# Experts of a mixture layer taken slice by slice in turn: three with 128 slots, five with 64 slots in plain fp32

## The chip, the cores and the metric

The kernel runs on one core of a Trainium2 chip. The metric is device time in microseconds (us) of one execution. A core has five engines that work side by side, each through its own instructions in order: PE (matmuls; PEld is its weight load), DVE and ACT (element-wise work), POOL, and SP, whose queue issues the transfers (DMA) from the chip's memory. Tiles lie in 128 partitions; accumulators of PE lie in eight banks (PSUM), one tile of 128 x 512 fp32 each.

## The reference, cut to what matters

Two layers run over 256 latent tokens of width 1024 and 256 context tokens. The end of the second layer, and 352 of the 490 MB that the program loads, is a mixture of eight experts of which each token uses two:

```python
def moe_ffn(h, w_router, b_router, w1, w3, w2):
    logits = (h @ w_router).astype(jnp.float32) + b_router.astype(jnp.float32)
    top_v, top_i = lax.top_k(logits, TOP_K)          # TOP_K = 2, N_EXPERTS = 8
    gates = jax.nn.softmax(top_v, axis=-1)
    comb = jnp.sum(jax.nn.one_hot(top_i, N_EXPERTS, dtype=jnp.float32) * gates[..., None], axis=-2)
    ...
    for e in range(N_EXPERTS):
        y = y + comb[..., e:e + 1] * swiglu(h, w1[e], w3[e], w2[e])
    return y

def swiglu(h, w1, w3, w2):                           # w1, w3: 1024 x 3584, w2: 3584 x 1024
    return (jax.nn.silu(h @ w1) * (h @ w3)) @ w2
```

## The kernel before, in words

The first part of the program (attention, dense layer, recurrent block) ends near 965 us of the profiled execution and is not touched. Then the router's scores are made (`lg`), each token's two experts are found, `asg` (token x expert, 0 or 1), `pos` (the token's place in its expert's list, by a matmul with a triangle) and `cnt` (how many tokens an expert has) are computed, and the experts follow.

An expert's hidden width of 3584 is cut into `NST` = 7 slices of 512. A slice has 12 units of weights, 128 x 1024 fp32 or 512 KB each: four of w1, four of w3 and four of w2. `up` computes both products of a slice, ACT takes Silu of the first (`msil`), DVE multiplies, PE transposes the result (`pgt`), and `w2_step` multiplies it by w2 one slice later, so that in slice n stand the w1 and w3 of slice n and the w2 of slice n - 1, then the transposes of slice n (`hidden`).

There are two kinds of expert. A *heavy* one has room for 128 tokens (slots). Its operands are split into two fp32r parts each: ACT casts a unit (`whi`, L354), DVE subtracts (`wlo`, L365), and PE makes three products (L1880 to L1882, and L1813 to L1815 for w2). The raw buffer of a unit is free once DVE has subtracted; up to `SB` = 5 units are split ahead. A *light* one (`LIGHT`) has `CAP` = 64 slots and multiplies in plain fp32 (L1793): two matmuls of 64 columns of weights work side by side on the two halves of the array, nothing is split, and the raw buffer is free only after its matmuls. Expert 0 is always the first, heavy; experts 1 to 7 are sorted by the length of their lists (`sort`, on DVE), the three longest are heavy, the four shortest light, and `RANK` deals them out alternately: heavy, light, heavy, light and so on, each with its seven slices in one piece.

Tokens are collected by matmuls with a 0/1 matrix: `gather` (eight per heavy expert) and `small_gather` (eight for all light ones together, into `xs`), after `picks` and `small_picks` on DVE. `turn` transposes an expert's matrix, `lift` scales its result, and `combine` (four per expert) adds it to the tokens. These are put into `side`, from which `step()` takes one piece after every second pair of units, four times per slice.

The class `Stream` loads the units in the order in which PE will want them. `load` issues transfers on SP as long as a raw buffer is free; SP then waits, in order, until the buffer's former user is done. Later tiles (`xs`, `xe`, `ysb`) lend their space to the stream before they are needed (`AG`). Which expert a load reads is taken from `order`, the sorted table, through a register (`expert`).

## Time and profile before

| | |
|---|---|
| time, median of 3 runs (lowest, highest) | 1849.22 us (1842.72, 1854.35) |
| the profiled execution | 1849.13 us, of which the span of its records is 1847.4 us |
| PE busy | 1770.6 us, 96% of the span |
| DVE busy | 1185.7 us, 64% |
| ACT busy | 859.7 us, 47% |
| DMA | 489.92 MB, mean 265 GB/s over the span |
| mean granted clock of PE | 0.981 of full |

All times inside the program count from the span's start. In rows of instructions, the first number is the start, the second the duration, both in us; `x4` is a count of merged instructions; the bracket names how long the engine stood idle before, and what ended that. `out<-in` are the program's names for tiles.

### The profile page before, as it was taken

How to read it: one execution, taken by the hardware profiler on the slowest of the kernel's cores; microseconds unless marked ns; L12 is line 12 of the kernel's file. 1: busy time of each engine (PE TensorE's matmuls, PEld its weight loads, DVE VectorE, ACT ScalarE, POOL GpSimd, SP SyncE). 2: the span in 40 equal slices, each digit the busy share in tenths (PEclk: the TensorE clock that was granted, in tenths of full speed). 3: DMA queues.
4: the chain of work that ended last, by engine and by line, in shares of the span. 5: the costliest groups of instructions: out<-in, count | busy, mean ns of one | idle time of the engine just before them, and what ended most of it. 6: DMA issues, size and time to landing. Idle time of an engine off the chain costs nothing.

```text
span 1847.4 us, 26663 instructions
## 1 busy us (share of the span) xinstructions
PE 1770.6 (96%) x10067; PEld 1357.1 (73%) x10067; DVE 1185.7 (64%) x1751; ACT 859.7 (47%) x1263; POOL 189.3 (10%) x195
## 2 busy tenths in 40 slices
PE   8999899999999999998778999999999999999996
PEld 6887568888788889877677886578755886578753
DVE  4784676876666448699987882188614983088611
ACT  4434655422222235776735762177413771167500
POOL 1001242100000003244650000000000000000000
PEclk9999999999999999999887999999999999999999
DMA  7444611464665323232565979999999999999996
GB/s 304 163 150 147 206 58 46 160 209 148 235 217 193 100 83 115 80 103 91 195 249 189 355 279 387 418 419 420 419 419 420 419 420 416 420 420 419 415 419 281
DMA packets 95257, 489.92 MB, mean 265 GB/s; under 512 B 10512, under 2 KB 16016, under 8 KB 56464
## 3 DMA queue, kind: packets, MB, share of 16 engines
q1 hardware_dynamic: 94976, 488.01, 68.4%
q8 instruction: 81, 1.33, 0.3%
q14 instruction: 56, 0.46, 0.1%
q10 hardware_dynamic: 144, 0.13, 0.0%
HBM read 487.05 MB, written 1.05 MB: 264 GB/s over the span
## 4 chain that ended last, share of the span: by engine, by line
PE 76%; DVE 11%; DMA 8%; ACT 2%; issue 2%; POOL 1%; SPq 0%; DVEq 0%; ACTq 0%; POOLq 0%
PE ph L1793 8%; DMA raw<-moe_d 7%; PE ph L1882 5%; PE ph L1880 5%; PE ph L1881 5%; PE psa L454 4%; PE psa L455 4%; PE psa L456 4%; PE py L1793 3%; PE py L1813 3%; PE py L1815 3%; PE py L1814 3%; DVE wlo L365 2%; PE pF L454 2%; PE pF L455 2%; PE pF L456 2%
## 5 line engine op out<-in xcount | busy, mean ns | idle before, releaser
L365 DVE TENSOR_TENSOR wlo<-raw,whi 128x1024 fp32r<-128x1024 f32 x480 | 575.4, 1237 | 158.5 <-ACT whi L354 157.1
L354 ACT CAST whi<-raw 128x1024 fp32r<-128x1024 f32 x484 | 490.9, 1048 | 206.5 <-PE pF L455 49.8
L1793 PE MATMUL ph<-raw,xs 128*64 128x256 f32 x1792 | 207.7, 383 | 1.4 <-DMA raw<-moe_d 1.4
L1882 PE MATMUL ph<-wlo,xe 128*128 128x512 f32 x448 | 178.4, 398 | 6.0 <-DVE wlo L365 6.0
L1880 PE MATMUL ph<-whi,xe 128*128 128x512 f32 x448 | 180.8, 404 | 2.5 <-ACT whi L354 2.5
L1881 PE MATMUL ph<-whi,xe 128*128 128x512 f32 x448 | 177.4, 396 | 0.0
L1793 PEld LDWEIGHTS ph<-raw,xs 128*64 128x64 f32 x1792 | 123.3, 137 | 65.3 <-issue 4.5
L454 PE MATMUL psa<-hh,whi 128*128 128x512 f32 (+1 forms) x384 | 144.8, 377 | 0.0
L455 PE MATMUL psa<-hl,whi 128*128 128x512 f32 (+1 forms) x384 | 143.9, 375 | 0.7 <-DVE hl L705 0.6
L456 PE MATMUL psa<-hh,wlo 128*128 128x512 f32 (+1 forms) x384 | 143.4, 373 | 0.0
L1793 PE MATMUL py<-raw,mgs 128*64 128x512 f32 (+1 forms) x496 | 103.4, 556 | 5.0 <-DMA raw<-moe_d 4.5
L579 DVE SCALAR_TENSOR_TENSOR macc<-raw,c,macc 128x1024 f32<-128x1024 f32 x84 | 105.3, 1280 | 0.7
L1882 PEld LDWEIGHTS ph<-wlo,xe 128*128 128x128 f32 x448 | 85.9, 192 | 26.3 <-DVE wlo L365 7.6
L1910 DVE TENSOR_TENSOR msil<-msil,ph 128x256 f32<-128x256 f32 x28 | 11.8, 420 | 144.1 <-PE ph L1793 144.1
L1880 PEld LDWEIGHTS ph<-whi,xe 128*128 128x128 f32 x448 | 86.2, 192 | 20.0 <-ACT whi L354 3.0
L1881 PEld LDWEIGHTS ph<-whi,xe 128*128 128x128 f32 x448 | 86.2, 192 | 17.3
L1813 PE MATMUL py<-whi,mgh 128*128 128x512 f32 x224 | 87.6, 391 | 0.0
L1815 PE MATMUL py<-wlo,mgh 128*128 128x512 f32 x224 | 87.3, 390 | 0.0
L1814 PE MATMUL py<-whi,mgl 128*128 128x512 f32 x224 | 87.2, 389 | 0.0
L454 PEld LDWEIGHTS psa<-hh,whi 128*128 128x128 f32 x384 | 73.0, 190 | 14.3 <-issue 2.1
L455 PEld LDWEIGHTS psa<-hl,whi 128*128 128x128 f32 x384 | 73.1, 190 | 13.6 <-DVE hl L705 1.5
L456 PEld LDWEIGHTS psa<-hh,wlo 128*128 128x128 f32 x384 | 73.1, 190 | 12.7
(351 smaller groups left out, 3235.8 us busy)
## 6 DMA issues: line engine op xcount, KB each, us to landing
raw<-moe_d SPq DMA_DIRECT2D x302, 1024.0 KB, 15.3
raw<-f_d SPq DMA_DIRECT2D x66, 512.0 KB, 3.6
raw<-wm_d SPq DMA_DIRECT2D x64, 512.0 KB, 4.7
raw<-moe_d SPq DMA_DIRECT2D x64, 512.0 KB, 15.7
raw<-wmh_d SPq DMA_DIRECT2D x32, 512.0 KB, 8.1
raw<-qkv_d SPq DMA_DIRECT2D x24, 512.0 KB, 4.4
raw<-win_d SPq DMA_DIRECT2D x24, 512.0 KB, 3.6
raw<-gat_d SPq DMA_DIRECT2D x14, 512.0 KB, 3.7
```

The source lines that it names most:

```text
L354: self.nc.scalar.copy(hi, self.raws[i][0])
L365: eng.tensor_tensor(lo, self.take(key), hi.bitcast(F32), ALU.subtract)
L454: nc.tensor.matmul(o, w[0], x[0], start=first, stop=False)
L455: nc.tensor.matmul(o, w[0], x[1], start=False, stop=False)
L456: nc.tensor.matmul(o, w[1], x[0], start=False, stop=last)
L1793: nc.tensor.matmul(o[h], x, w[h], start=first, stop=last, skip_group_check=True)
L1813: nc.tensor.matmul(ys[e][n], x[0], w[0], start=b, stop=False)
L1814: nc.tensor.matmul(ys[e][n], x[1], w[0], start=False, stop=False)
L1815: nc.tensor.matmul(ys[e][n], x[0], w[1], start=False, stop=l)
L1880: nc.tensor.matmul(acc[part], xh[:, k], w[0], start=(k == 0), stop=False)
L1881: nc.tensor.matmul(acc[part], xl_[:, k], w[0], start=False, stop=False)
L1882: nc.tensor.matmul(acc[part], xh[:, k], w[1], start=False, stop=(k == 7))
```

## The change

The numbers of kinds and the order change. `FEW` = 5 experts are light, three are heavy, and `order` is used as sorted: places 0, 1 and 2 are heavy (expert 0 and the two longest lists), 3 to 7 light. Slices are no longer taken expert by expert: `turns` lists all 56 slices, first three of expert 0, then the 35 light ones in order with the other 18 heavy ones spread between them: `h h h l l h l l h l l h l l h l l h l h l l h ...`, with three light ones at the end. Heavy and light experts are thus open at the same time, so the accumulators are no longer taken from rotating pools: `bank` hands three banks round for w1 and w3, a light slice puts both of its halves of 256 columns into one of them, a fourth bank holds the light w2 sums and two hold the heavy ones.

As the first light loads come early, `sort` runs ahead of the first gathers, the rest of it (`permute`) after slice 0 as before, and the count of tokens is made beside `pos`. `gate` holds back loads that need `order` until `sort` has been written. `xs` and `ysb` lend less space. The small gathers, now 320 columns wide, move from slices 4 and 5 into slice 2, three per `step()`. `combine` of an expert starts two places after its last slice.

```diff
-RANK = (None, 3, 0, 4, 1, 5, 2, 6)
-LIGHT = (1, 3, 5, 7)
+FEW = 5
+HEAVY = tuple(range(NE - FEW))
+LIGHT = tuple(range(NE - FEW, NE))
+
+
+def turns():
+    h, l = ([(e, s) for e in k for s in range(NST)] for k in (HEAVY, LIGHT))
+    q = h[:3]
+    h = h[3:]
+    n = len(h)
+    for i, x in enumerate(l):
+        q.append(x)
+        while h and len(h) > n - n * (i + 1) // (len(l) - 3):
+            q.append(h.pop(0))
+    return q
+
+
+SEQ = turns()
...
-AG = (1,1)
+AG = (0, 1)
...
-        while self.dma_at < len(self.units) and n:
+        while self.dma_at < (len(self.units) if self.gate is None else self.gate) and n:
...
-    for p in range(NE):
-        for s in range(NST):
...
+    for n, (p, s) in enumerate(SEQ):
+        if p and st.gate is None:
+            st.gate = len(st.units)
...
-                once = [mp.tile([P, 2, UNIT], F32, name="raw", tag=n, bufs=b) for n, b in (("xs", 1), ("xe", 2))]
-                st.add_tiles(once, 2 * AG[0], True)
-                st.add_tiles([mp.tile([P, UNIT], F32, name="raw", tag="ysb", bufs=1)], AG[1])
+                once = mp.tile([P, max(2 * UNIT, KD * CAP * FEW)], F32, name="raw", tag="xs", bufs=1)
+                st.add_tiles([once[:, 0:2 * UNIT].rearrange("p (i n) -> p i n", i=2)], AG[0], True)
+                st.add_tiles([mp.tile([P, 2, UNIT], F32, name="raw", tag="xe", bufs=2)], AG[1], True)
...
+    nc.tensor.matmul(pp[:, 16:24], ones, asg[:, 0], start=False, stop=False)
+    nc.tensor.matmul(pp[:, 16:24], ones, asg[:, 1], start=False, stop=True)
...
+    sort()
+    st.gate = None
+    for k in range(KD):
+        gather(0, k)
...
+    banks_a, banks_u, turn_a = [psa("ph") for _ in range(4)], [psu("py") for _ in range(2)], [0]
+
+    def bank():
+        turn_a[0] += 1
+        return banks_a[turn_a[0] % 3]
...
     def step():
-        if side:
-            side.pop(0)()
+        for _ in range(rate[0]):
+            if side:
+                side.pop(0)()
...
-        acc = [psa("ph")[:, 0:NL], psa("ph")[:, 0:NL]]
+        acc = bank()
+        acc = [acc[:, 0:NL], acc[:, NL:512]]
...
+    for n, (e, s) in enumerate(SEQ):
+        while after and after[0][0] <= n:
+            p = after.pop(0)[1]
+            side[:0] = [lambda p=p, c=c: combine(p, c) for c in range(4)]
...
+        if n == 2:
+            side += [lambda t=t: small_picks(t) for t in range(2)]
+            side += [lambda k=k: small_gather(k) for k in range(KD)]
+        rate[0] = 3 if n == 2 else 1
+        sil = (small_up if e in LIGHT else up)(e, s)
...
```

Three places show how instructions move. On SP, the loads (`raw<-moe_d`) that stand ahead of the first use of `order`, and the first behind it; before, the table's first use comes 28 loads further on. Before, from the second load into a lent tile on:

```order
L289 DMA raw<-moe_d 128x2048 [waits DMAHW7_49]
L276 DMA raw<-moe_d 128x1024 [waits DMAHW0_49,DVE_49]
L276 DMA raw<-moe_d 128x1024 [waits DMAHW1_49]
L289 DMA raw<-moe_d 128x2048 [waits DMAHW2_49,DVE_49]
L289 DMA raw<-moe_d 128x2048 [waits DMAHW3_49,Pool_49]
L289 DMA raw<-moe_d 128x2048 [waits DMAHW4_49,PE_49]
L289 DMA raw<-moe_d 128x2048 [waits DMAHW5_49,DVE_49]
```

The change, from the same load on:

```order
L306 DMA raw<-moe_d 128x2048 [waits DMAHW7_49]
L306 DMA raw<-moe_d 128x2048 [waits DMAHW0_49,DVE_49]
L306 DMA raw<-moe_d 128x2048 [waits DMAHW1_49,Pool_49]
L306 DMA raw<-moe_d 128x2048 [waits DMAHW2_49,PE_49]
L306 DMA raw<-moe_d 128x2048 [waits DMAHW3_49,DVE_49]
L797 TENSOR_LOAD order [waits DVE_49]
```

The pair of half-size loads into a raw buffer and the lent `ysb` is gone, so that each later load stands behind a release of a buffer that is one pair of units later; and SP now reads `order` here.

On DVE, the start of the experts. Before, the eight subtractions of the first gathers follow the parts `hnl` of the tokens at once, and the sort (`key` to `order`) stands behind slice 0:

```order
L1643 TENSOR_SCALAR Pm<-con,pos,asg 128x128 x2
L1614 SCALAR_TENSOR_TENSOR hnl<-pR,nry,hnh 128x512 x3
L1667 SCALAR_TENSOR_TENSOR xe<-pg,mods_78,xe 128x128 x8
L1702 COPY cnt<-pcnt 128x8
L365 TENSOR_TENSOR wlo<-raw,whi 128x1024 x7
```

The change:

```order
L1657 COPY cnt<-ppos 128x8
L1662 TENSOR_SCALAR Pm<-con,pos,asg 128x128 x2
L1631 SCALAR_TENSOR_TENSOR hnl<-pR,nry,hnh 128x512 x3
L1719 TENSOR_SCALAR key<-con 128x8
L1720 SCALAR_TENSOR_TENSOR key<-cnt,key 128x8
L1722 TENSOR_TENSOR above<-key 128x49
L1724 TENSOR_REDUCE rank<-above 128x7
L1725 TENSOR_TENSOR perm<-rank,con 128x49
L1726 MEMSET srt 128x16
L1727 TENSOR_TENSOR permv<-perm,con 128x49
L1728 TENSOR_REDUCE srt<-permv 128x7
L1729 CAST order<-srt 128x8
```

Nine instructions stand between the tokens' parts and the eight `xe` subtractions now.

On PE, the w1 and w3 matmuls of a light slice (`ph<-raw,xs`; the waits for `DMAHW` are for loaded units). Before, the last two pairs of units and the first of w2:

```order
L1793 MATMUL ph<-raw,xs 64x256 [waits DMAHW7_49]
L1793 MATMUL ph<-raw,xs 64x256 x7
L1793 MATMUL ph<-raw,xs 64x256 [waits DMAHW0_49]
L1793 MATMUL ph<-raw,xs 64x256 x7
L1793 MATMUL py_10153<-raw,mgs 64x512 [waits DMAHW1_49,Activation_49]
```

The change, in a light slice behind a heavy one:

```order
L1816 MATMUL ph<-raw,xs 64x256 [waits DMAHW6_49]
L1816 MATMUL ph<-raw,xs 64x256 x3
L1816 MATMUL ph<-raw,xs 64x256 [waits DMAHW7_49,Activation_49]
L1816 MATMUL ph<-raw,xs 64x256 x7
L1836 MATMUL py<-whi,mgh 128x512
```

The last pair of w3 units waits for ACT as well.

## Rows read from the trace of the kernel before

**Rows 1.** The page: the DMA engines' share and rate in 40 equal slices.
```profile
DMA  7444611464665323232565979999999999999996
GB/s 304 163 150 147 206 58 46 160 209 148 235 217 193 100 83 115 80 103 91 195 249 189 355 279 387 418 419 420 419 419 420 419 420 416 420 420 419 415 419 281
```

**Rows 2.** DMA issues from 900 us on: count, KB of each, us to landing.
```profile
raw<-moe_d SPq DMA_DIRECT2D x302, 1024.0 KB, 15.3
raw<-moe_d SPq DMA_DIRECT2D x64, 512.0 KB, 15.7
raw<-w2l_d SPq DMA_DIRECT2D x4, 512.0 KB, 14.3
```

**Rows 3.** Stretches: us, busy us (count) of five engines, PE clock, DMA share, GB/s.
```profile
912.00:1037.00 125.00, 108.41 (x601) 96.27 (x600) 106.47 (x166) 71.39 (x100) 32.07 (x23) 0.86 0.64 247
1037.00:1045.00 8.00, 8.00 (x39) 6.65 (x38) 6.09 (x7) 5.41 (x7) 0.00 (x0) 1.00 1.04 368
1037.00:1115.00 78.00, 77.06 (x387) 63.13 (x387) 61.88 (x64) 52.35 (x62) 0.00 (x0) 1.00 0.81 298
1120.00:1800.00 680.00, 674.72 (x3881) 468.06 (x3881) 369.67 (x425) 311.50 (x397) 0.00 (x0) 0.99 1.01 419
1825.00:1832.00 7.00, 5.53 (x36) 2.09 (x32) 0.35 (x1) 0.74 (x2) 0.00 (x0) 1.00 0.67 266
1005.00:1010.00 5.00, 3.12 (x7) 2.48 (x8) 4.93 (x9) 1.04 (x1) 0.00 (x0) 0.50 0.18 29
```

**Rows 4.** Waits of SP's queue from 982 to 1115: us in total, times, longest.
```profile
SPq L289 <- DVE wlo L365: 108.2, 30, 16.2
```

**Rows 5.** Timeline of PE: transposes at the end of heavy (L1859) and light (L1854) slices.
```profile
1037.01 0.60 PE L1859 MATMUL pgt<-con,msil 128*128 128x128 f32 x4
...
1109.52 0.60 PE L1859 MATMUL pgt<-con,msil 128*128 128x128 f32 x4
...
1197.88 0.44 PE L1854 MATMUL pgt<-con,msil 128*128 128x128 f32 x2
...
1300.20 0.60 PE L1859 MATMUL pgt<-con,msil 128*128 128x128 f32 x4
...
1317.01 0.60 PE L1859 MATMUL pgt<-con,msil 128*128 128x128 f32 x4
...
1790.45 0.44 PE L1854 MATMUL pgt<-con,msil 128*128 128x128 f32 x2
...
1801.31 0.44 PE L1854 MATMUL pgt<-con,msil 128*128 128x128 f32 x2
```

**Rows 6.** Timeline: the sort on DVE (first row, row behind its last), PE's stop.
```profile
999.36 0.17 DVE L1724 TENSOR_SCALAR key<-con 128x8 f32<-128x8 f32 x1
...
1001.06 0.20 DVE L1738 TENSOR_TENSOR permv<-perm,cnt 128x49 f32<-128x49 f32 x1
...
1006.88 0.79 PE L1882 MATMUL ph<-wlo,xe 128*128 128x512 f32 x1 [4.90 <-DVE wlo L365]
```

**Rows 7.** Timeline of PE: small gathers, the first and the second.
```profile
1063.66 0.39 PE L1684 MATMUL pg<-Ps,hnh 128*128 128x256 f32 x1 [0.94 <-DVE Ps L1643]
...
1066.84 0.40 PE L1684 MATMUL pg<-Ps,hnh 128*128 128x256 f32 x2
...
1067.32 0.40 PE L1813 MATMUL py<-whi,mgh 128*128 128x512 f32 x1
```

**Rows 8.** Groups by line and form: ACT's casts and the light slices' Silu.
```profile
L354 ACT CAST whi<-raw 128x1024 fp32r<-128x1024 f32 x484 | 490.9, 1048 | 206.5 <-PE pF L455 49.8 <-issue 46.1 <-DMA raw<-moe_d 35.8
...
L1908 ACT ACTIVATE msil<-ph 128x256 f32<-128x256 f32 x28 | 10.8, 385 | 85.8 <-PE ph L1793 85.8
```

**Rows 9.** Timeline of the end: ACT's last copy, w2 behind it, last addition.
```profile
1829.61 0.37 ACT L1856 COPY mgs<-pgt 128x256 f32<-128x256 f32 x1 [7.55 <-PE pgt L1854]
...
1830.03 1.09 PE L1793 MATMUL py<-raw,mgs 128*64 128x128 f32 x16 [0.52 <-ACT mgs L1856]
...
1839.64 0.48 DVE L730 SCALAR_TENSOR_TENSOR xl<-pc,mods,xl 128x256 f32<-128x256 f32 x1 [0.59 <-PE pc L1830]
```

More of the change, by code (lines that the diff above doesn't have):

```diff
@@ L1635, in body @@
     nc.tensor.matmul(pp[:, 0:16], tri, asg.rearrange("p t e -> p (t e)"), start=True, stop=False)
-    nc.tensor.matmul(pp[:, 0:16], ones, asz[:, 0:2].rearrange("p t e -> p (t e)"), start=False, stop=True)
+    nc.tensor.matmul(pp[:, 0:16], ones, asz[:, 0:2].rearrange("p t e -> p (t e)"), start=False, stop=False)
+    nc.tensor.matmul(pp[:, 16:24], ones, asg[:, 0], start=False, stop=False)
+    nc.tensor.matmul(pp[:, 16:24], ones, asg[:, 1], start=False, stop=True)
     nc.vector.tensor_copy(pos, pp[:, 0:16].rearrange("p (t e) -> p t e", t=2))
+    nc.vector.tensor_copy(cnt, pp[:, 16:24])
     xe, PT, pms = {}, {}, {}
-    col = [0] + [1 + RANK[p] for p in range(1, NE)]
     def hot(o, slots, p, t, gate=None):
-        c = col[p]
+        c = p
         nc.vector.tensor_scalar(
@@ L1672, in small_picks @@
         if t == 0:
-            small["P"] = mp.tile([P, 2, 4, CAP], F32R, name="Ps", bufs=1)
+            small["P"] = mp.tile([P, 2, FEW, CAP], F32R, name="Ps", tag="ysb", bufs=1)
         for j, p in enumerate(LIGHT):
@@ L1678, in small_gather @@
         if k == 0:
[L1679 removed]
+            small["x"] = mp.tile([P, KD, FEW, CAP], F32, name="xs", tag="xs", bufs=1)
         g = pst("pg")
@@ L1757, in sort, with weights @@
         nc.gpsimd.memset(small["PT"].bitcast(F32), 0.0)
+    warm(W3, wz, pst)
+    picks(0)
+    for low in lows[1:]:
+        low()
+    sort()
+    st.gate = None
+    for k in range(KD):
+        gather(0, k)
+    st.widen(zr, 3)
+    st.hold = False
+    st.flush()
+    banks_a, banks_u, turn_a = [psa("ph") for _ in range(4)], [psu("py") for _ in range(2)], [0]
+    def bank():
+        turn_a[0] += 1
+        return banks_a[turn_a[0] % 3]
+    def weights():
+        g1 = tp.tile([P, 2, 2], F32, name="g12", bufs=1)
+        dn = tp.tile([P, 2], F32, name="dn", bufs=1)
+        nc.vector.tensor_scalar(dn, e2, 1.0, None, ALU.add)
+        nc.vector.reciprocal(g1[:, 0], dn)
+        nc.vector.tensor_tensor(g1[:, 1], e2, g1[:, 0], ALU.mult)
+        for t in range(2):
+            nc.vector.tensor_scalar(comb[:, t], oh[:, 0, t], g1[:, 0, t:t + 1], None, ALU.mult)
+            nc.vector.scalar_tensor_tensor(comb[:, t], oh[:, 1, t], g1[:, 1, t:t + 1], comb[:, t], ALU.mult, ALU.add)
+    fold_d = [None]
     gs = {}
@@ L1862, in hidden @@
         prev[0] = (e, s, gt)
-    side = []
+    side, rate, after = [], [1], []
     def step():
-        if side:
-            side.pop(0)()
+        for _ in range(rate[0]):
+            if side:
+                side.pop(0)()
     def up(e, s):
-        acc = [psa("ph"), psa("ph")]
+        acc = [bank(), bank()]
         xh, xl_ = xe[e]
@@ L1903, in small_up @@
                     (acc[part][0:CAP], acc[part][CAP:P]), x[:, k, j],
-                    [u[:, kk * 512 + h * NL:kk * 512 + h * NL + NL] for h in range(2)], k == 0, k == 7,
+                    [u[:, kk * 512 + h * NL:kk * 512 + h * NL + NL] for h in range(2)], k == 0 and part == 0, k == 7 and part == 1,
                 )
@@ L1914, in small_up @@
         return sil
-    for e in range(NE):
-        for s in range(NST):
-            if s == 1 and e > 0:
-                side += [lambda e=e, c=c: combine(e - 1, c) for c in range(4)]
-            if s == 2:
-                side.append(lambda e=e: turn(e))
-            if s == 4 and e == 0:
-                side += [lambda t=t: small_picks(t) for t in range(2)]
-                side += [lambda k=k: small_gather(k) for k in range(KD)]
-            if s == 3 and e % 2 and e + 1 < NE:
-                side.append(lambda p=e + 1: picks(p))
-                side += [lambda p=e + 1, k=k: gather(p, k) for k in range(KD)]
-            sil = (small_up if e in LIGHT else up)(e, s)
-            if (e, s) == (0, 0):
-                weights()
-                sort()
-                side.append(lambda: hidden(0, 0, sil))
-                continue
-            w2_step()
-            hidden(e, s, sil)
+    for n, (e, s) in enumerate(SEQ):
+        while after and after[0][0] <= n:
+            p = after.pop(0)[1]
+            side[:0] = [lambda p=p, c=c: combine(p, c) for c in range(4)]
+        if s == 2:
+            side.append(lambda e=e: turn(e))
+        if s == 3 and e + 1 in HEAVY:
+            side.append(lambda p=e + 1: picks(p))
+            side += [lambda p=e + 1, k=k: gather(p, k) for k in range(KD)]
+        if n == 2:
[3 more added lines that the diff above has]
+        sil = (small_up if e in LIGHT else up)(e, s)
+        if s == NST - 1:
+            after.append((n + 2, e))
+        if n == 0:
+            weights()
+            permute()
+            side.append(lambda: hidden(0, 0, sil))
+            continue
+        w2_step()
+        hidden(e, s, sil)
     e, s, gt = prev[0]
```

74 lines of the change are left out of this document (24 added, 50 removed).

## The prediction

> **What bounds the kernel now.** I read the tenths in 40 slices first. PE is at 9 nearly everywhere, but ends of matmuls are modelled, so the DMA row is the harder evidence: it stands at 9 from the twenty-fourth slice to the last but one, with 387 to 420 GB/s [rows 1]. What is loaded there is the experts' weights, 302 pieces of 1 MB and 64 + 4 of 512 KB [rows 2]: 2 x 302 + 68 = 672 units of 512 KB, 352.3 MB. From 1120 to 1800 they come at 419 GB/s with the engines' share at 1.01 [rows 3]. One unit then costs 0.5243 / 419 = 1.251 us, and all of them 841 us. So compute that gets faster does not shorten the last 700 us; transfers that come earlier do.
>
> Where are they late? The table by stretch [rows 3] gives 125 us x 247 GB/s = 30.9 MB from 912 to 1037, 0.5 MB of it the last unit of w_out: 58 units. From 1037 to 1115 at 298 GB/s come another 44, 102 in all; 570 units at 1.251 us then end at 1828. The row from 1825 to 1832 agrees: 7 x 266 / 419 = 4.4 us of transfer, so the loads end at 1829.4. From 1037 to 1115 the kernel loses 78 x (1 - 298/419) = 22.5 us of transfer. The queue's own waits say why: of the 133 us from 982 to 1115 SP waits 108 for `wlo`, the subtraction that frees a raw buffer [rows 4]. Expert 0 is heavy: PE uses a heavy slice's 12 units in 16.8 us (1300.20 to 1317.01), where the DMA needs 15.0, and a light slice's in 10.9 (1790.45 to 1801.31) [rows 5]. So the buffers stay full for seven heavy slices, and the queue saturates only when the first light expert empties them.
>
> **What the change does, step by step.** The transfers stay 672 units. What moves is where light slices begin: after three heavy slices (1037) and not after seven (1109.52 [rows 5]).
>
> *The start of the light slices, t3.* Before, the third heavy slice's transposes start at 1037.01 [rows 5]. The sort: nine DVE instructions, from 999.36 up to 1001.06, leave a chain behind which PE stood for 4.90 us, to 1006.88 [rows 6]. They now go ahead of the eight `xe` subtractions, whose gathers have four banks to run ahead in, so I cost them at nothing there (uncovered: 1.7 us). PE's stop shrinks by 1.7 us. The clock was granted at 0.50, the lower level of 1.2 GHz, from 1005 to 1010 after that stop [rows 3]; if the shorter stop spares this, another 2 us are saved. I take 2.5 of 1.7 to 3.7. The count of tokens costs two matmuls more ahead and four less behind: nothing. Against it, the eight small gathers come from slices 4 and 5 into slice 2, three per step. One takes 0.48 us (1066.84 to 1067.32) at 256 columns [rows 7]; at 320, 0.6, so 4.7 us. The first waited 0.94 us for its picks [rows 7]; with ten picks, 1. The third of a burst needs a bank that ACT empties behind a cast of 1.05 us [rows 8]: 0 to 1 us at each of two bursts, I take 0.4. Together 6.5 us. t3 = 1037 - 2.5 + 6.5 = 1041, between 1038 and 1045.
>
> *What has landed by then.* The old code holds some 28 units between the oldest raw buffer in use and the newest load; the borrowed tiles `ysb` and `xs` are lent less now (the order shows SP's loads ahead of `order` one pair short), which leaves 24 to 26. At t3 PE has used 8 + 12 + 12 = 32 units. Before, five more were split by then and their buffers free: 32 + 5 + 28 = 65 issued, 58 landed. Now the next units are light ones, which keep their buffer up to their matmuls: 32 + 24 = 56 issued, landed about 3 us later, at 1044. The new kernel is behind there; it gains afterwards, at the full rate where the old one ran at 298 GB/s.
>
> *From 1044 on.* 616 units at 1.251 us are 771 us, if PE empties buffers that fast. PE's need: 18 heavy slices at 16.8 and 35 light ones at 10.9 are 684 us. Side work: from 1109.52 to 1197.88 seven light slices took 88.4 [rows 5] against 7 x 10.9 + 2 (one heavy w2 for a light one) = 78, so 10 us for eight gathers, a turn and a heavy combine; the next seven, heavy, to 1317.01, took 119.1 against 7 x 16.8 - 2 = 115.6, so 3.5 for a light combine and turn. Two sets of gathers, three heavy and four or five light combines make about 39. Sum 723.
>
> *The new wait.* A light slice now has both accumulators in one bank, and in the order PE's last pair of w3 units waits for ACT, that is for Silu on the w1 half. The old trace has no such wait. Lower bound: the nearest round trip from PE to ACT and back, 0.52 us idle around a copy of 0.37 [rows 9]; Silu takes 0.385 [rows 8]. Upper bound: a whole cast ahead of Silu in ACT's queue besides, 1.05 us [rows 8], 1.6 in all. Behind the waiting matmul stand the w2 of the slice before and the transposes, and behind these the buffers that SP waits for. I take 1.0, since casts fill ACT only near heavy slices: 35 us over 35 light slices. PE then needs 758 (741 to 779) against the DMA's 771, which still sets the end.
>
> The Trainium skill speaks for the wait: its page "PSUM — Partial Sum Buffer", section "PSUM bank collisions raise a hardware error", asks that TensorE's write and another engine's read of one bank be kept apart by a semaphore, whichever columns they touch. By that rule the wait has to be paid in every light slice; without it PE's need would be 723 us. No run so far shows a collision.
>
> *The ramp.* With few loads in flight the rate is lower, 368 GB/s from 1037 to 1045 [rows 3]; over some 25 us that costs 25 x (1 - 368/419) = 3 us.
>
> *The end.* From the end of the loads, 1829.4, to the span's end, 1847.4, are 18.0 us: the last transposes, four column blocks up to 1839.64 and the output [rows 9]. That code stays.
>
> Sum: 1041 + 3 + 771 + 3 + 18 = 1836 us of span. The profiled execution took 1849.13 with a span of 1847.4, so 1.7 us lie around it, and it stands at the median of 1849.22. Prediction: **1838 us**, 0.6% faster.
>
> The Trainium skill's page "DMA: Bandwidth & Descriptors", section "Specifications", gives about 358 GB/s as HBM's limit for one core and 435 as the fabric's ceiling. The trace's 419 over 680 us [rows 3] contradicts the first, and the measurement decides. As an estimate by the second, 616 units would take 742 us and the end would be near 1809; no long stretch of this trace comes near it.
>
> **The rivals.**
> (a) *PE becomes the bound*, through the shared bank and through casts that wait for a transfer ahead of Silu; this one ends slower or barely faster. For it: ACT works in order and already waited 35.8 us for raw loads [rows 8]. Against it: when PE falls behind, buffers fill and ACT no longer waits for loads. The end is then t3 + 723 + waits + 18. It decides from 48 us of waits (1.4 per light slice), equals the old time at 65 (1.9), and at 2.2 per slice gives 1041 + 723 + 77 + 18 + 1.7 = 1861; above 1867.7 it needs 2.4.
> (b) *The queue saturates earlier*: the gathers hide behind DVE's subtractions, the clock does not fall, and four more units are loaded. t3 = 1037, 60 landed by 1040: 1040 + 612 x 1.251 + 18 + 1.7 = 1825. For it: in that slice DVE has as much to do as PE, so PE has some gaps. Against it: the gathers are 4.7 us of PE's own work.
> (c) *The change does not do what it says*, since the third-longest list of experts 1 to 7 does not fit 64 slots and the overflow branch reads that expert again: 84 units, 105 us, 1943. Against it: the reference on its own inputs sends 126, 79, 62, 44, 43, 40 and 36 tokens to them and 82 to expert 0, so the list fits by two.
>
> **Chances.** With this kernel a difference under about 1% (18.5 us: 1830.7 to 1867.7) can hardly be told from none. The forecast, DMA-bound, ending between 1831 and 1850: 0.64. Rival (b), below 1831: 0.18. Rival (a): 0.17, of which 0.12 lies between 1850 and 1868 and 0.05 above. Rival (c): 0.01. So faster by over 1%: 0.18; within 1%: 0.76; slower: 0.06. The range, 1824 to 1856, leaves out about 0.07 of (b) and 0.11 of (a) and (c).
>
> **What would show it.** Right: 419 GB/s from about 1050 to 1815 in the table by stretch, some 56 units ahead of that, the third transposes of expert 0 near 1041, and about 1 us of PE idle behind Silu in each light slice. Wrong: a DMA share well below 1 after 1060 (then PE is the bound, and its waits for ACT and DVE say by what), or third transposes much later than 1045.

## The result, and the profile after

The changed kernel takes 1836.67 us (median of 8 runs, 1831.38 to 1839.83), the kernel before, run beside it, 1847.55 us (8 runs, 1842.72 to 1854.35): a ratio of 0.994, 95% interval 0.9926 to 0.9953. That is 10.9 us, 0.6% less: inside the 1% that the prediction calls the same, and resolved by this many runs. The forecast was 1838 us. The profiled execution took 1835.84 us, of which 1834.1 are its span.

The page's two DMA rows, in 40 slices of 45.9 us, answer to [rows 1]:

```profile
DMA  8444621454655323232365799999999999999996
GB/s 307 164 157 142 202 63 47 143 204 159 230 206 208 105 86 116 85 103 93 140 258 203 282 419 419 420 419 420 419 421 419 419 420 419 420 420 420 419 420 272
```

The full rate now begins with the twenty-fourth slice (1054.6); before, the twenty-sixth was the first at 418. Up to the last but one it never falls below 419.

The table by stretch (columns as in [rows 3]):

```profile
912.00:1037.00 125.00, 109.11 (x633) 96.70 (x632) 106.67 (x175) 72.44 (x106) 31.45 (x23) 0.90 0.61 232
1037.00:1044.00 7.00, 7.00 (x58) 4.89 (x58) 1.92 (x2) 1.53 (x2) 0.00 (x0) 1.00 0.38 144
1044.00:1060.00 16.00, 15.03 (x110) 10.10 (x106) 3.83 (x4) 5.45 (x8) 0.00 (x0) 1.00 1.00 397
1060.00:1800.00 740.00, 704.71 (x4176) 458.76 (x4174) 328.82 (x378) 268.94 (x360) 0.00 (x0) 0.99 1.01 419
1812.00:1819.00 7.00, 6.05 (x46) 2.69 (x42) 0.42 (x1) 0.69 (x2) 0.00 (x0) 1.00 0.54 219
1002.73:1006.00 3.27, 3.27 (x8) 2.59 (x9) 3.27 (x4) 1.04 (x1) 0.00 (x0) 0.50 0.27 60
```

From these, as in the prediction: 125 x 232 = 29.0 MB less 0.5 of w_out are 54.4 units by 1037, 7 x 144 = 1.0 MB make it 56.3 by 1044, and 16 x 397 another 12.1 by 1060, 68.4 in all. The loads end at 1812 + 7 x 219/419 = 1815.7. Behind that lie 18.4 us to the span's end. The last row is PE's first work behind its stop (the 3.15 us below): the clock is at its lower level there.

PE's timeline around the start of the light slices: transposes of slices 0, 1 and 2 (heavy, L1882), then of the first two light ones (L1877), and PE's stop behind slice 0:

```profile
995.76 0.60 PE L1882 MATMUL pgt<-con,msil 128*128 128x128 f32 x4
...
1002.73 0.79 PE L1906 MATMUL ph<-wlo,xe 128*128 128x512 f32 x1 [3.15 <-DVE wlo L382]
...
1014.81 0.60 PE L1882 MATMUL pgt<-con,msil 128*128 128x128 f32 x4
...
1038.52 0.60 PE L1882 MATMUL pgt<-con,msil 128*128 128x128 f32 x4
...
1052.38 0.38 PE L1877 MATMUL pgt<-con,msil 128*128 128x128 f32 x2
...
1063.89 0.44 PE L1877 MATMUL pgt<-con,msil 128*128 128x128 f32 x2
```

Slice 1 takes 19.05 us and slice 2, with the small gathers, 23.71. Of before, the same timeline has:

```profile
998.19 0.60 PE L1859 MATMUL pgt<-con,msil 128*128 128x128 f32 x4
...
1019.46 0.60 PE L1859 MATMUL pgt<-con,msil 128*128 128x128 f32 x4
```

With 1037.01 [rows 5] these were 21.27 and 17.55 us.

Waits of the changed kernel from 1041 on (total, times, longest):

```profile
ACT whi L371 <- DMA raw<-moe_d: 102.2, 49, 7.7
...
PEld ph L1816 <- ACT msil L1933: 48.0, 31, 4.9
PE ph L1816 <- ACT msil L1933: 33.9, 31, 4.4
```

PE's idle time behind Silu comes to 33.9 us, as forecast (35). But ACT's wait for loads has gone from 35.8 us [rows 8] to 102.2, and the longest of PE's waits, 4.4 us, is far more than the 1.6 that the prediction set as the most of one. One place shows how they hang together (ACT's timeline, then PE's):

```profile
1329.11 1.04 ACT L371 CAST whi<-raw 128x1024 fp32r<-128x1024 f32 x1 [6.44 <-DMA raw<-moe_d]
1330.06 0.38 ACT L1933 ACTIVATE msil<-ph 128x256 f32<-128x256 f32 x1
```

```profile
1330.49 3.49 PE L1816 MATMUL ph<-raw,xs 128*64 128x256 f32 x16 [3.11 <-ACT msil L1933]
```

A cast stands ahead of Silu in ACT's queue and waits 6.44 us for its transfer. PE's row names Silu, but what was late was the load. So the 33.9 us are no price of the shared bank alone; the experiments take them apart.

### The profile page after: what moved, and what is told of

It is laid out like the page before. It is cut to its first block, busy times and chain, and to the rows that moved or that the text cites. A ratio compares the mean times of both kernels' runs of the same rounds, so it can differ in the third digit from the quotient of the medians.

```text
span 1834.1 us, 26274 instructions
## 1 busy us (share of the span) xinstructions
PE 1732.2 (94%) x10069; PEld 1290.6 (70%) x10069; DVE 1084.9 (59%) x1653; ACT 767.3 (42%) x1171; POOL 188.3 (10%) x195
## 2 busy tenths in 40 slices
DMA packets 94965, 489.89 MB, mean 267 GB/s; under 512 B 10480, under 2 KB 15984, under 8 KB 55920
## 4 chain that ended last, share of the span: by engine, by line
PE 60%; DMA 22%; DVE 12%; ACT 3%; issue 2%; POOL 1%; SPq 0%; DVEq 0%; ACTq 0%; POOLq 0%
DMA raw<-moe_d 21%; PE ph L1816 10%; PE psa L471 4%; PE psa L472 4%; PE psa L473 4%; DVE wlo L382 3%; PE ph L1906 2%; PE ph L1904 2%; PE ph L1905 2%; PE pF L471 2%; PE pF L472 2%; PE pF L473 2%; PE py L1836 1%; PE py L1837 1%; PE py L1838 1%
## 5 line engine op out<-in xcount | busy, mean ns | idle before, releaser
L382 DVE TENSOR_TENSOR wlo<-raw,whi 128x1024 fp32r<-128x1024 f32 x396 | 481.5, 1240 | 219.7 <-ACT whi L371 215.0
L371 ACT CAST whi<-raw 128x1024 fp32r<-128x1024 f32 x400 | 407.3, 1046 | 252.3 <-DMA raw<-moe_d 102.2
L1816 PE MATMUL ph<-raw,xs 128*64 128x256 f32 x2240 | 267.0, 390 | 33.9 <-ACT msil L1933 33.9
L1906 PE MATMUL ph<-wlo,xe 128*128 128x512 f32 x336 | 132.8, 395 | 4.6 <-DVE wlo L382 4.6
L1904 PE MATMUL ph<-whi,xe 128*128 128x512 f32 x336 | 134.0, 399 | 0.3 <-ACT whi L371 0.3
L1905 PE MATMUL ph<-whi,xe 128*128 128x512 f32 x336 | 131.7, 392 | 0.0
L1816 PE MATMUL ph<-raw,mgs 128*64 128x512 f32 (+1 forms) x608 | 127.9, 562 | 0.5 <-ACT mgs L1879 0.5
L1816 PEld LDWEIGHTS ph<-raw,mgs 128*64 128x64 f32 x608 | 40.7, 137 | 67.6 <-issue 62.8
L471 PE MATMUL pF<-gh,whi 128*128 128x512 f32 (+1 forms) x208 | 74.8, 360 | 0.4 <-ACT gh L484 0.4
L472 PE MATMUL pF<-gl,whi 128*128 128x512 f32 (+1 forms) x208 | 74.3, 357 | 0.3 <-DVE gl L485 0.3
L473 PE MATMUL pF<-gh,wlo 128*128 128x512 f32 (+1 forms) x208 | 74.2, 356 | 0.0
```

The lines of the kernel that those rows point to most:

```text
L371: self.nc.scalar.copy(hi, self.raws[i][0])
L382: eng.tensor_tensor(lo, self.take(key), hi.bitcast(F32), ALU.subtract)
L471: nc.tensor.matmul(o, w[0], x[0], start=first, stop=False)
L472: nc.tensor.matmul(o, w[0], x[1], start=False, stop=False)
L473: nc.tensor.matmul(o, w[1], x[0], start=False, stop=last)
L1816: nc.tensor.matmul(o[h], x, w[h], start=first, stop=last, skip_group_check=True)
```

## The experiments

The theory is that of the prediction: transfers set the end, so what counts is how early they run at full rate. The standing rival is TensorE as the bound. A light slice frees its buffers without VectorE and with less of PE's time, so two things could bring the gain: that light slices come earlier, or that there are more of them.

**The number alone.** Five light experts, worked expert by expert.

```diff
-SEQ = turns()
+SEQ = [(e, s) for e in (0, 3, 1, 4, 2, 5, 6, 7) for s in range(NST)]
...
-        if s == 3 and e + 1 in HEAVY:
+        if s == 3 and e in (3, 4):
...
```

> The changed kernel with five 64-slot experts, but worked through expert by expert: expert 0 in seven heavy slices first, then 3, 1, 4, 2, 5, 6, 7 by rank. It has the new number and not the new order. Theory (the transfers set the end, and the gain is their earlier start at full rate): the raw buffers stay full until expert 0 is through near 1112, some 102 units have landed at 1115, the other 570 at 1.251 us end near 1828, and the time is that of before, 1848 us (1843 to 1853). Rival (TensorE sets the end, and the gain is that seven heavy slices became light): it has the same slices as the changed kernel, so 1837 us.

Measured: 1845.34 us, ratio to before 0.9986 (0.9971 to 1.0). By the medians the number alone brings 2.0 us, by the interval between 0 and 5.4: nothing that is clear of noise. Its table by stretch:

```profile
1037.00:1060.00 23.00, 23.00 (x107) 19.02 (x107) 20.45 (x20) 17.83 (x20) 0.00 (x0) 1.00 0.88 327
1060.00:1115.00 55.00, 54.52 (x276) 43.80 (x276) 41.33 (x39) 35.61 (x40) 0.00 (x0) 1.00 0.90 344
1115.00:1800.00 685.00, 645.15 (x3928) 405.52 (x3924) 267.56 (x328) 225.48 (x309) 0.00 (x0) 1.00 1.01 419
```

Until expert 0 is through, the rate stays at 327 to 344 GB/s; only then comes 419. PE has 40 us to spare in the third row and they buy nothing. That PE's work fell by seven slices is worth next to nothing where the transfers set the end. This run has the rest of the change too (the earlier sort, the small gathers in slice 2, the shared bank), so these do not bring the gain by themselves either.

**The order alone.** Four light experts, slice by slice.

```diff
-FEW = 5
+FEW = 4
```

> The changed kernel with four 64-slot experts in place of five, in the new order (three heavy slices, then light and heavy ones in turn). It has the new order and not the new number. Theory: the transfers start at full rate as early as in the changed kernel, and TensorE now needs 25 heavy slices x 16.8 + 28 light ones x 11.5 + 39 of side work = 781 us from the third transposes (792 with 1.0 us of wait per light slice in place of 0.6), against 773 for the transfers; so most of the gain stays, 1838 to 1849, likeliest 1841 us. Rival (the gain comes from the number of light slices): none of it stays, 1848 us or more.

Measured: 1850.35 us, ratio 1.0015 (1.0001 to 1.0028). That is 1.4 us over the theory's range, and nothing of the gain stays. The chain that ended last (the work followed back from the last instruction, at each step to what released it, in shares of the span), of the changed kernel first and of this one second:

```profile
PE 60%; DMA 22%; DVE 12%; ACT 3%; issue 2%; POOL 1%; SPq 0%; DVEq 0%; ACTq 0%; POOLq 0%
```

```profile
PE 81%; DVE 11%; ACT 3%; issue 2%; DMA 1%; POOL 1%; SPq 0%; DVEq 0%; POOLq 0%; ACTq 0%
```

The DMA's share of the chain falls from 22% to 1%: PE has become the bound. The mechanism was in the expectation (781 to 792 us of PE's time against 773), its size was low by some 12 us. The reason is in the timeline: light and heavy slices in turn took

```profile
1114.67 0.38 PE L1877 MATMUL pgt<-con,msil 128*128 128x128 f32 x2
1129.50 0.66 PE L1882 MATMUL pgt<-con,msil 128*128 128x128 f32 x4
```

14.83 us for the heavy one, and 13.94 for the light one behind it (to 1143.44), together 28.8, where I had added 16.8 + 11.5 = 28.3 from slices that follow their like. 25 such pairs are 12 us more: 781 + 12 = 793 us, and 1037.5 + 793 + 18 + 1.7 = 1850. So the order brings the transfers forward, and without the fifth light expert PE can't follow them. Its loads end near 1824, some 24 us before the span's end and not 18 (in the row from 1819 to 1826 they still run at 276 GB/s, in the next 7 us at 4). Neither half alone brings a gain that is clear of noise, both together 10.9 us.

**The Silu wait away.** Two banks for the halves of a light slice again.

```diff
-        acc = bank()
-        acc = [acc[:, 0:NL], acc[:, NL:512]]
+        acc = [bank()[:, 0:NL], bank()[:, 0:NL]]
...
-                    [u[:, kk * 512 + h * NL:kk * 512 + h * NL + NL] for h in range(2)], k == 0 and part == 0, k == 7 and part == 1,
+                    [u[:, kk * 512 + h * NL:kk * 512 + h * NL + NL] for h in range(2)], k == 0, k == 7,
```

> The changed kernel, but the two halves of a light slice's accumulator lie in two banks again, so that the w3 matmuls need not wait for Silu. Theory: the 34 us in which TensorE stood behind Silu go, and the time does not move, since the transfers from 1044 on take the same 771 us: 1837 us (1834 to 1840), and TensorE waits for loads instead. Rival (TensorE sets the end): about 34 us less, 1803 us.

Measured: 1837.10 us, ratio 0.9936 (0.9913 to 0.9958): no change. Its waits from 1041 on have no row of a matmul behind Silu, and ACT's wait for loads has grown from 102.2 to

```profile
ACT whi L371 <- DMA raw<-moe_d: 143.5, 64, 7.5
```

The time that was not lost behind Silu was lost behind the transfers. Two light slices in a row stood 11.51 us apart in the changed kernel (1052.38 to 1063.89); here it is

```profile
1053.42 0.38 PE L1877 MATMUL pgt<-con,msil 128*128 128x128 f32 x2
1064.22 0.44 PE L1877 MATMUL pgt<-con,msil 128*128 128x128 f32 x2
```

10.80: here, where no load is late, the shared bank costs 0.7 us.

**The cover away.** A light slice loads two of its four w2 units and uses the second one three times. 70 units are not loaded, PE's work is the same, and the result is another.

```diff
-            for i in range(4):
+            for i in range(2 if SEQ[n - 1][0] in LIGHT else 4):
                 add_moe(("w2", *SEQ[n - 1], i), 8)
...
-            u = st.need(("w2", e, s, f))
+            if e not in LIGHT or f < 2:
+                u = st.need(("w2", e, s, f))
...
```

> The changed kernel without the third and fourth w2 unit of each light slice: the matmuls use the second unit again, 70 units (36.7 MB, 88 us at 419 GB/s) are not loaded, TensorE's work is the same. Theory: the transfers then need 771 - 88 = 683 us and TensorE sets the end with its 744 to 758 us: 1038.5 + 744 to 758 + 18.8 + 1.7 = 1803 to 1817 us, so that the loss of cover behind the Silu wait shows. Rival (TensorE sets the end already): no change, 1837 us. Second rival (the transfers would set the end with much more room under them, since TensorE's slices of before were already stretched by loads): down to 1837 - 88 = 1749 us.

Measured: 1806.47 us, ratio 0.9765 (0.974 to 0.979), in the theory's range: 88 us of transfer less shortened the kernel by 30 and no more. Those 30 us are the room that PE has under the transfers. The waits behind Silu, now that loads are early:

```profile
PEld ph L1816 <- ACT msil L1935: 29.1, 31, 0.9
PE ph L1816 <- ACT msil L1935: 15.0, 31, 0.5
```

As many of them as before, but none longer than 0.5 us on PE: 18.9 of the 33.9 us of idle time were transfer time under another name.

**Cover and wait away.** Both edits at once; again two w2 units of each light slice are left out.

```diff
-            for i in range(4):
+            for i in range(2 if SEQ[n - 1][0] in LIGHT else 4):
...
-        acc = bank()
-        acc = [acc[:, 0:NL], acc[:, NL:512]]
+        acc = [bank()[:, 0:NL], bank()[:, 0:NL]]
...
```

> The changed kernel without the third and fourth w2 unit of each light slice (70 units are not loaded, the second is used again) and with the halves of a light slice in two banks, so without the wait for Silu. Theory: with the cover of the transfers gone the wait costs what it takes, 0.7 us per light slice by the distance of two light slices' transposes with and without it (11.5 and 10.8 us), so 35 x 0.7 = 25 us less than with the shared bank (1806.5): 1782 us (1776 to 1790). Rival (the wait is only a label, and TensorE would stand elsewhere for the same time): 1806 us.

Measured: 1779.11 us, ratio 0.9633 (0.9614 to 0.9651). Against the run with the shared bank these are 27.4 us by the medians and 24.4 by the ratios; from the first transposes to the end the two profiles differ by 21.8 (806.8 and 785.0). That makes 0.6 to 0.8 per light slice. So the wait is real and costs this much per slice where PE sets the end; in the changed kernel the transfers hide all of it. The price is more than the 15.0 us that PE's row calls idle, so the row of a wait alone does not give it; the weight loads (PEld) stood 29.1 us behind Silu in that run.

**More work for PE.** Idle matmuls behind each light slice, two and six.

```diff
+        warm(2, hn_h[:, 0], pst)
         return sil
```

> The changed kernel with two idle matmuls of 512 columns behind each light slice, 35 x 2 x 0.233 = 16 us more of TensorE's time (0.233 us is a heavy slice's 16.8 over its 72 matmuls). Theory: TensorE alone would be through 30 us earlier than the transfers (1837 against the 1806.5 with fewer loads), so that 16 us are hidden: 1837 us (1835 to 1841). Rival (TensorE sets the end): 1853 us.

Measured with two: 1840.64 us, ratio 0.9968 (0.9955 to 0.9981). Of 16 us some 12 are hidden; 4 show, the upper edge of what the theory allowed.

```diff
+        warm(6, hn_h[:, 0], pst)
         return sil
```

> The changed kernel with six idle matmuls of 512 columns behind each light slice, 35 x 6 x 0.233 = 49 us more of TensorE's time. Theory: 30 us of it are hidden, 19 show: 1806.5 + 49 = 1856 us (1852 to 1862). Rival (TensorE sets the end): 1886 us. If the transfers hid it all: 1837 us.

Measured with six: 1855.13 us, ratio 1.0052 (1.0036 to 1.0069), on the forecast. 49 us more of PE's work cost 18.5. The chain's DMA share goes the same way: 22% in the changed kernel, 13% with two, 2% with six. Where the 4 us of the first dose come from is not settled: as much had landed 65 us behind the first transposes as in the changed kernel (the table below), and the rate from 1060 to 1800 is 418 for 419, which makes 1.8 us.

**Light slices one slice earlier.** Two heavy slices ahead of them, the small gathers in slice 1, and the tile `xs` no longer lent to loads.

```diff
-    q = h[:3]
-    h = h[3:]
+    q = h[:2]
+    h = h[2:]
...
-                st.add_tiles([once[:, 0:2 * UNIT].rearrange("p (i n) -> p i n", i=2)], AG[0], True)
...
-        if n == 2:
+        if n == 1:
             side += [lambda t=t: small_picks(t) for t in range(2)]
...
```

> The changed kernel with the light slices one slice earlier: two heavy slices ahead of them in place of three, the ten picks and eight small gathers in the second slice, and the tile of the small gathers not lent to the loads (two units fewer land ahead). Theory: transfers run at full rate from about 1024 in place of 1044; some 46 units have landed by then in place of 57, the other 626 at 1.251 us are 783: 1024 + 4 + 783 + 18.8 + 1.7 = 1831 us (1828 to 1836). Rival (the small gathers now wait for the permutation on VectorE behind the first slice, and TensorE stands for what is won): 1837 us or more.

Measured: 1837.37 us, ratio 0.994 (0.9922 to 0.9959): as the changed kernel, the rival's number. PE's timeline has the rival's wait, too:

```profile
1007.91 0.64 PE L1702 MATMUL pg<-Ps,hnh 128*128 128x320 f32 x1 [6.48 <-DVE Ps L1661]
```

The light slices began at 1026.20, behind the 1024 at which the expectation already had the full rate. SP had also stood once for 25.8 us, for the sort, since the first unit that needs it comes twelve units sooner. Which of them ate the gain?

**The sort's wait away.** The same kernel, with experts loaded by their own numbers; the weights are then not those that the tokens want.

```diff
-        return lambda: a["moe"][(expert(p) if p else 0, *i)]
+        return lambda: a["moe"][(p, *i)]
...
```

> The kernel with two heavy slices ahead of the light ones, but the experts are loaded by their own numbers and not by rank, so that no load waits for the sort (the queue stood 25.8 us for it); the experts' weights are then not those of the tokens, all work is the same. Theory (full buffers: 20 used + 24 held = 44 units at the start of the light slices whatever came before, as in the run with the sort, where 43.7 had landed by 1030): the wait was made up before 1010, and the time stays at 1837 us (1835 to 1839). Rival (the wait for the sort ate the gain): 25.8 us less of standing give 1829 to 1832 us.

Measured: 1836.03 us, ratio 0.994 (0.9918 to 0.9963). The wait for the sort cost nothing; it was made up while the buffers had room. The table by stretch explains it, cut at the first transposes, 45.3 us behind them and another 19.7 (the changed kernel first, then the one with two heavy slices and the sort's wait):

```profile
900.76:995.76 95.00, 80.38 (x490) 73.02 (x491) 84.79 (x121) 57.81 (x89) 39.48 (x29) 0.86 0.52 198
995.76:1041.06 45.30, 41.46 (x203) 33.59 (x203) 33.95 (x67) 26.11 (x34) 0.00 (x0) 0.96 0.65 247
1041.06:1060.76 19.70, 18.73 (x140) 12.43 (x138) 4.83 (x6) 6.21 (x9) 0.00 (x0) 1.00 0.93 368
```

```profile
903.07:998.07 95.00, 80.38 (x490) 73.05 (x491) 84.79 (x121) 57.88 (x89) 39.47 (x29) 0.86 0.45 175
998.07:1043.37 45.30, 37.83 (x219) 29.16 (x219) 23.67 (x57) 16.18 (x23) 0.00 (x0) 0.92 0.71 275
1043.37:1063.07 19.70, 19.22 (x111) 13.08 (x108) 9.78 (x9) 9.35 (x13) 0.00 (x0) 1.00 1.01 417
```

In units, 35.9 + 21.3 + 13.8 = 71.0 against 31.7 + 23.8 + 15.7, which is 71.1 before rounding: another way to the same place. My expectation had counted the gain wrongly. A heavy slice uses 12 units in 16.8 us where the transfers need 15.0, so by estimate putting one behind the light slices is worth 1.8 us. The light slices began 28.1 us behind the first transposes; the 42.8 of the changed kernel less 16.8 are 26.0. The difference, 2.1 us, which holds the 6.48 us stop, spends the gain.

**A lent tile fewer.** Only `xs` no longer lent.

```diff
-                st.add_tiles([once[:, 0:2 * UNIT].rearrange("p (i n) -> p i n", i=2)], AG[0], True)
```

> The changed kernel without the tile that it lends to the loads until the small gathers need it: 2 units fewer are in the buffers when the light slices begin, nothing else. Theory of the landed units (while heavy slices run, the buffers are full, and what has landed is what TensorE has used plus what the buffers hold): 2 x 1.251 = 2.5 us later, 1839.5 us (1838 to 1842). Rival (in that stretch the queue is limited by its rate and not by buffers): no change, 1837 us.

Measured: 1836.12 us, ratio 0.9933 (0.9917 to 0.9949): no change, the theory's 2.5 us did not come.

```profile
903.65:998.65 95.00, 80.38 (x491) 73.10 (x492) 84.76 (x121) 57.81 (x89) 39.50 (x29) 0.86 0.49 187
998.65:1043.95 45.30, 41.40 (x201) 33.61 (x201) 33.87 (x67) 26.09 (x34) 0.00 (x0) 0.96 0.72 270
```

Two units fewer have landed by the first transposes (33.9 for 35.9), and 45.3 us later as many as in the changed kernel (57.2 and 57.2). The loan is over by then in both, since the small gathers take the tile back; what counts is how much the buffers hold when the light slices begin, and that is the same.

**VectorE's chain dealt out.** PE's stop behind slice 0 comes from 5.8 us of small VectorE instructions in one piece. Here they go in three pieces between the subtractions of slice 1.

```diff
         if n == 0:
-            weights()
-            permute()
             side.append(lambda: hidden(0, 0, sil))
+            side += [lambda: (weights(), count()), lambda: permute((asg, pos)), lambda: (permute((comb,)), rest_())]
...
```

> The changed kernel with the small VectorE instructions behind the first slice (weights, counts, permutation of three tables, 5.8 us in one piece) dealt out over three steps of the second slice, so that the subtractions that TensorE waits for go between them. TensorE's stop of some 5 us near 1000 should all but go, and the third transposes come 4 to 5 us earlier. Theory (full buffers: until the light slices begin, TensorE's pace sets how much has landed, so a stop there shifts everything behind it one to one): 1837 - 4.5 = 1832.5 us (1831 to 1834). Rival (the transfers go on at some 235 of 419 GB/s meanwhile, and only the rest of the stop is lost): 2 us less, 1835 us.

Measured: 1837.01 us, ratio 0.9941 (0.9926 to 0.9957): neither the theory nor the rival. The stop moved. Slice 1 shrank from 19.05 to 16.79 us, slice 2 grew from 23.71 to 27.71. VectorE is why; from 1000 to 1024, in the changed kernel and in this one:

```profile
1000.00:1024.00 24.00, 20.60 (x90) 16.78 (x91) 23.35 (x37) 15.27 (x19) 0.00 (x0) 0.93 0.70 264
```

```profile
1000.00:1024.00 24.00, 19.50 (x86) 14.57 (x85) 23.23 (x56) 14.36 (x19) 0.00 (x0) 0.98 0.66 251
```

It is busy for 23 of 24 us (the third busy time of a row) in both: a heavy slice's own subtractions all but fill it, so what the chain no longer cost PE in slice 1 it cost in slice 2. What was saved at 1002 was paid in slice 2, where PE waited for the picks,

```profile
1021.05 0.38 PE L1703 MATMUL pg<-Ps,hnh 128*128 128x320 f32 x1 [1.47 <-DVE Ps L1662]
1022.07 0.41 PE L1703 MATMUL pg<-Ps,hnh 128*128 128x320 f32 x1 [0.64 <-DVE Ps L1662]
```

and its clock fell right behind them:

```profile
1023.00:1026.00 3.00, 3.00 (x11) 2.51 (x10) 1.29 (x2) 2.00 (x4) 0.00 (x0) 0.50 0.50 158
```

Since the third transposes came 44.5 us behind the first and not 42.8, so no earlier, what an earlier start is worth, one to one or less, was not tried by this run.

**Gathers behind the start.** Dealt out as above, and in slice 2 only the first light expert's tokens are gathered.

```diff
...
+            side += [lambda k=k: small_gather(k, 0, 1) for k in range(KD)]
+        if n == 3:
+            side += [lambda t=t: small_picks(t, range(1, FEW)) for t in range(2)]
+            side += [lambda k=k: small_gather(k, 1) for k in range(KD)]
...
```

> The kernel with the dealt-out VectorE instructions, and besides only the first light expert's tokens (64 columns in place of 320) are gathered in the third slice; those of the other four (256 columns) follow in the fourth to sixth, behind the start of the light slices, where TensorE has some 30 us to spare. Theory: the third slice is 8 gathers x (0.6 - 0.2) us = 3 us shorter, one to one again: 1829.5 us (1828 to 1832). Rival (the gathers are hidden there, or eight gathers cost the same at 64 columns as at 320): no less than with the dealt-out instructions alone.

Measured: 1838.76 us, ratio 0.9952 (0.9934 to 0.997): no gain. The timeline of the start:

```profile
1036.53 0.60 PE L1886 MATMUL pgt<-con,msil 128*128 128x128 f32 x4
1051.00 0.38 PE L1881 MATMUL pgt<-con,msil 128*128 128x128 f32 x2
1065.06 0.44 PE L1881 MATMUL pgt<-con,msil 128*128 128x128 f32 x2
```

The third transposes did come sooner, 41.8 us behind the first and not 42.8 (the theory: 3 us by the split alone). But the first two light slices then took 14.5 and 14.1 us in place of 13.9 and 11.5: the work came back at once, and more. Right behind the start PE has no room yet; from 975 to 1120 SP's queue of the changed kernel waits 39.1 us for light matmuls to free a buffer, so there PE's pace still is the transfers'. What landed by 65 us is the same (71.4 and 71.0 units), and that the median is 2 us above the changed kernel is not resolved by these intervals.

All runs together. The first transposes of expert 0 start anywhere from 992.7 to 998.7 in these profiles, scatter that lies ahead of the slices, so the third column is measured from there to the span's end. The last is what landed from 95 us ahead of them to 65 behind, in units of 512 KB; it is worked out from rates rounded to 1 GB/s and good to 0.2.

| kernel | median us | first transposes to end | landed |
|---|---|---|---|
| before | 1847.55 | 849.2 | 77.3 |
| changed | 1836.67 | 838.3 | 71.0 |
| number alone | 1845.34 | 847.4 | 71.2 |
| order alone | 1850.35 | 851.4 | 71.5 |
| two banks | 1837.10 | 838.2 | 71.1 |
| fewer loads | 1806.47 | 806.9 | 71.4 |
| fewer loads, two banks | 1779.11 | 785.0 | 70.9 |
| PE +16 us | 1840.64 | 841.7 | 71.3 |
| PE +49 us | 1855.13 | 859.5 | 70.9 |
| two heavy ahead | 1837.37 | 838.4 | 71.1 |
| the same, no sort | 1836.03 | 839.3 | 71.2 |
| `xs` not lent | 1836.12 | 839.4 | 70.6 |
| dealt out | 1837.01 | 839.8 | 69.6 |
| dealt out, split | 1838.76 | 841.5 | 71.4 |

None that does all the work is measurably faster than the changed kernel. Whatever was done ahead of the light slices, 69.6 to 71.5 units have landed 65 us behind the first transposes. The number alone has its 71, too, and loses its 9 us behind that point, at 344 GB/s. The kernel before is six units ahead there and still ends 11 us later, as the prediction had it: behind at first, gaining at the full rate.

## Why the prediction was right

Point by point, forecast and trace:

| step | forecast | changed kernel |
|---|---|---|
| slice 1, by the earlier sort and the clock | -2.5 us | -2.2 (21.27 to 19.05) |
| slice 2, by the small gathers | +6.5 us | +6.2 (17.55 to 23.71) |
| third transposes | 1041 | 1038.5 |
| third transposes, counted from the first | 42.8 us | 42.8 |
| landed 3 us behind the third transposes | 56 units (1044) | 55.2 (1041.5) |
| from those 3 us on to the end of the loads | 771 + 3 = 774 us | 774.2 |
| PE idle behind Silu | 35 us, 1.0 per slice | 33.9 |
| from the end of the loads to the span's end | 18.0 us | 18.4 |
| span | 1836 | 1834.1 |
| from the first transposes to the span's end | 837.8 us | 838.3 |

**The bound.** Transfers set the end: one unit costs 1.251 us from 1060 on, the time does not move when PE has 34 us less to wait, and it does when 70 units are not loaded. The Trainium skill's page "DMA: Bandwidth & Descriptors", section "Specifications", gives about 358 GB/s as HBM's limit for one core. The changed kernel's 419 over 740 us is over that, as it was before. The forecast by the trace's rate, 774 us with the ramp, met 774.2. (One reading is off by a slice: before, the DMA's tenths stand at 9 from the twenty-fifth slice on, where 387 GB/s stands, and not from the twenty-fourth [rows 1]; no term of the sum uses it.)

**The start.** Both changes of pace were forecast within 0.3 us. The third transposes came 2.5 us before their forecast because the whole program had started its expert 0 that much earlier (995.76 for 998.19), which the runs show to be scatter between executions and no part of the change. Counted from the first transposes, sum and trace differ by 0.5 us; with a range of 1038 to 1045 for the third transposes alone, so close a match is luck in part. The stop behind slice 0 shrank from 4.90 to 3.15 us, the 1.7 us of the forecast. The clock was not spared: it fell to 0.50, the lower level of 1.2 GHz, in both kernels, but PE worked at it for 3.3 us (1002.73 to 1006) and before for some 4 us, from 1006.88 [rows 6] to 1011, as [rows 3] and this row of before show:

```profile
1010.00:1011.00 1.00, 1.00 (x4) 0.78 (x3) 1.00 (x2) 0.00 (x0) 0.00 (x0) 0.50 0.95 401
```

By estimate the clock thus gave back some 0.4 of the 2 us that the prediction had in question.

**The landed units.** 55.2 were there 3 us behind the third transposes, and 56.3 by 1044. The way to the number, used plus held, holds: taking a lent tile away or letting the queue stand 25.8 us changed nothing of it.

**The Silu wait.** That 33.9 us met the forecast of 35 is luck, and this term of the sum was sized too high. I had priced the shared bank at 1.0 us per light slice, 35 in all; where PE sets the end it costs 0.6 to 0.8, 22 to 27 in all. Of the 33.9 us of idle time in the changed kernel only some 15 are the bank's, and the others are time in which a cast ahead of Silu waits for its load. The time was forecast well all the same, since the transfers cover this term. The prediction named late casts under rival (a), with the remark that ACT does not wait for loads when PE falls behind; with fewer loads that is what the rows show, no wait over 0.5 us. The page "PSUM — Partial Sum Buffer" of the Trainium skill, section "PSUM bank collisions raise a hardware error", asks for a semaphore between one engine's write and another's read of a bank; by that rule the wait has to be paid in every light slice. The trace agrees as far as it goes: it has 31 such waits, and two banks for the halves take them away; no run here went without the semaphore on one bank.

**PE's room.** From the third transposes on, the forecast gave the transfers 3 + 771 + 3 = 777 us and PE 758, so 19 us were left to PE. It is 30. PE's need without the wait came out right (723 forecast; with two banks and fewer loads 1782.4 - 1040.3 - 18 = 724), in part because two errors cancel: in that run a light slice and a heavy one in turn took 13.2 + 14.8 = 28.0 us where 10.9 + 16.8 = 27.7 was counted, some 6 us over all slices at their shortest, and what is left for side work is 34.5 us and not 39. The wait was too dear by some 12 us (with one bank and fewer loads 1805.1 - 1041.0 - 18 = 746, forecast 758). Rival (a) was thereby further off than its 0.17 says; 49 us of added work, on top of the waits, took the kernel to 1855. Its threshold was set too low as well: by the prediction's own sum PE decides from 777 - 723 = 54 us of waits, not 48.

**The rivals.** (b) needed third transposes at 1037 and four more units; neither came, and the experiments that tried for an earlier start show why none was to be had cheaply. (c) did not occur: the changed kernel moved 489.89 MB, the one before 489.92, and 84 units more would be 44 MB.

What the prediction did not say is how narrowly the two halves of the change fit. By its own numbers four light experts in this order leave PE 7 x (16.8 - 11.9) = 34 us more to do, more than the room of 19 us, and five in the old order leave the transfers late. It priced the package and would have had to price each half to see that one without the other is worth next to nothing.

## What to carry to other kernels

Find the stretch from which the bound resource never rests again, and count what it has done by then; edits behind that point that only help the other engines are worth nothing until that cover is used up, and a run that takes work from the bound resource measures how thick the cover is. When a wait's row names an engine, look at what stood ahead in that engine's queue: here over half of PE's idle time behind Silu was waiting for loads. And where two parts of a change move two bounds that lie close together, price them apart: here neither alone brought a gain clear of noise, both 10.9 us.

## What the runs showed of the hardware

The granted clock fell to 0.50, the lower level of 1.2 GHz, from 1023 to 1026 in the run with the dealt-out chain, behind waits of PE of 1.47 and 0.64 us with one matmul between them. Behind a single stop of 3.15 us in the changed kernel it was at 0.50 from 1002.73 to 1006. In these two cases two short stops close together cost about as much of the clock as a longer one.

From 1060 to 1800 (with the number alone from 1115) the transfers gave 418 to 420 GB/s in every kernel in which they set the end. With 70 units fewer and PE as the bound the rate from 1060 to 1700 was 396, and 408 with two banks:

```profile
1060.00:1700.00 640.00, 625.95 (x3780) 409.50 (x3778) 290.94 (x340) 240.62 (x328) 0.00 (x0) 1.00 0.98 396
```

The DMA engines' share is 0.98 in this row though a good part of the loads is gone. With the order alone and with 49 us more for PE, where the chain names PE, the share from 1060 to 1800 is even 1.01, at 415 and 414 GB/s. A share near 1 does not by itself say that the transfers set the end. That the time moved when transfers were taken away says it.

A heavy slice behind a light one and a light one behind a heavy one took 28.8 us together, 0.5 more than slices that follow their like; what that half microsecond is was not looked into.
